# Softmax scores of 640 columns: 384 + 256 columns with two short ones to a bank, in place of 512 + 128 with four to a bank

## The chip, the cores and the metric

The kernel runs on one core of one Trainium2 chip. The metric is the device time of one execution in microseconds (us), the median of the runs shown. Below, PE is the matrix engine, PEld its weight loads, DVE the vector engine, ACT the scalar engine, POOL the GpSimd engine and SP the engine that issues most DMAs.

## The reference

One layer of an encoder on 2048 tokens of width 1024: a normed and modulated input, one projection, eight stick-breaking heads and eight softmax heads of 64 columns, an output projection, and a squared-ReLU MLP. The change is in the softmax heads, whose reference is, cut to what matters:

```python
s = jnp.einsum('bnqhd,bnkhd->bnhqk', qc, k_band).astype(jnp.float32) * (d ** -0.5)
bias = rel_bias[:, rel_idx].astype(jnp.float32)
s = s + bias[None, None]
s = jnp.where(valid[None, :, None, None, :], s, NEG_INF)
p = jax.nn.softmax(s, axis=-1)
out = jnp.einsum('bnhqk,bnkhd->bnqhd', p.astype(v.dtype), v_band)
```

A chunk has 64 queries and sees its own chunk and the 8 before it, 576 keys.

## The kernel before, in words

The kernel handles the tokens in reverse, and takes two chunks as one query tile of 128 rows. Such a tile sees a window of 640 keys (`WIN`), of which the bias masks the corner that each chunk does not see. Near the end of the reversed sequence fewer keys are left.

**Units.** The attention stage walks over units of four query tiles, one tile to a step. A softmax unit, class `CA`, is one head and one group of 512 queries; it is written (head, group) here. Groups 0, 1 and 2 have 640 keys for each of their four tiles. In group 3 the tiles have 512, 384, 256 and 128 keys. The units of groups 1, 2 and 3 of all heads run in one stretch of the program, those of group 0 in a later one, and stick-breaking units (`SB`) before and after the first stretch.

**Scores.** A query tile's scores are a matmul of 640 columns, done twice into the same place since the keys are kept as a high and a low part in one contraction and the query's two parts follow one another (`for l in range(2)`). A PSUM bank holds 512 fp32 columns, so the scores are split: the first `hn` columns go to a bank of the tile's own (names that begin with `cz`), the rest, here called the short part, to a bank that several tiles share (`ct`, `self.tails`). In the kernel before, `hn` is 512, the short part 128, and one `ct` bank takes the short parts of all four tiles, at the start of the unit (L972 to L978).

**What reads the banks.** DVE adds the bias to the short part and takes its minimum (`tail`, L992; the signs are turned, so it is the maximum of the scores), then does the same with the first `hn` columns from that minimum on (L1003). Each of the two is followed by a short instruction that reads the minimum out. ACT takes the exponentials of the 640 columns of SBUF with their sum, DVE the reciprocal, POOL scales.

**The rest of a step.** Eight steps later PE transposes the weights of that unit (`wt`), ACT and DVE split them into a high and a low part (`wth`, `wtl`), and PE multiplies them with the values (`acc`), some steps later still. Between the scores and the next step's transposes, PE gets fill matmuls of other layers' projections (`pf`, `po`), a share that is set by a credit for each step and not by the time.

**Order.** PE's instructions are kept in the order in which the program writes them (`Ordered`); so a PE instruction that waits holds back all that follows. In a step PE's order is transposes, values, the next tile's scores, fill. The other engines and the DMA queue are ordered by the scheduler of the framework, which also picks the bank of each tile. `cz`, `ct`, `wt` and the stick-breaking scores `z` share four PSUM banks (`pz`, tag `z`); a tile takes a bank that has come free and waits, on PE, for the instruction that frees it. In the profile nearly all lines are L42, since a helper records every operation, so names of tiles tell the work apart.

Of the kernel before, what the change touches and what calls it, by code (L numbers as in the profile page):

```python
# [9 lines left out]
F32 = mybir.dt.float32  # L10
# [8 lines left out]
P = 128  # L19
# [6 lines left out]
TB = 512  # L26
# [53 lines left out]
def encoder_kernel(ctx, tc, xT, x3, wf, c, g1, g2, w_in, w_rest, gqk, bias, w_o, w1, w2, w_ada, b_ada, out):  # L80
    nc = tc.nc
    act, dve, pool, sp = nc.scalar, nc.vector, nc.gpsimd, nc.sync
    pe = Ordered(tc, nc.tensor)
    osp = Ordered(tc, nc.sync)

    WIN = 640
# [8 lines left out]
    pz = ctx.enter_context(tc.tile_pool(name="pz", bufs=4, space=PSUM))  # L95
# [36 lines left out]
    def column(tag):  # L132
        small[tag].append(small[tag].pop(0))
        return small[tag][-1]
# [110 lines left out]
    if True:  # L245
# [304 lines left out]
        t = np_.tile([P, 4], F32, tag="nt", name="nta3")  # L550
# [200 lines left out]
    if True:  # L751
# [109 lines left out]
        class SB(Unit):  # L861
# [31 lines left out]
            def scores(self, qi):  # L893
                nm = f"{self.nm}_{qi}"
                c0 = qi * P if self.diag else 0
                n = TB - c0
                self.z = z = pz.tile([P, TB], F32, tag="z", name=f"z{nm}")
                qs = slice(qi * P, (qi + 1) * P)
                pe.matmul(z[:, :n], self.q[:, 0, qs], self.k[:, c0:], start=True, stop=False)
                pe.matmul(z[:, :n], self.q[:, 1, qs], self.k[:, c0:], start=False, stop=True)  # L900
# [28 lines left out]
        class CA(Unit):  # L929
# [34 lines left out]

            def size(self, qi):
                n = min(WIN, self.nk - qi * P)
                return n, min(n, TB)

            def scores(self, qi):
                nm = f"{self.nm}_{qi}"  # L970
                n, hn = self.size(qi)
                if qi == 0 and n > hn:  # L972
                    self.tails = pz.tile([P, TB], F32, tag="z", name=f"ct{nm}")
                    for i in range(STEPS):
                        t = self.tails[:, i * P : (i + 1) * P]
                        ks = slice(i * P + TB, i * P + WIN)
                        for l in range(2):
                            pe.matmul(t, self.q[:, l, i * P : (i + 1) * P], self.k[:, ks], start=l == 0, stop=l == 1)  # L978
                self.z = z = pz.tile([P, TB], F32, tag="z", name=f"cz{nm}")
                ks = slice(qi * P, qi * P + hn)  # L980
                for l in range(2):
                    pe.matmul(z[:, :hn], self.q[:, l, qi * P : (qi + 1) * P], self.k[:, ks], start=l == 0, stop=l == 1)

            def tail(self, qi):
                nm = f"{self.nm}_{qi}"
                n, hn = self.size(qi)
                s = zp.tile([P, WIN], F32, tag="p", name=f"s{nm}")
                m = 3e38
                if n > hn:
                    m = column("m0")  # L990
                    t = self.tails[:, qi * P : (qi + 1) * P]
                    dve.tensor_tensor_reduce(s[:, hn:n], t, self.bt[:, hn:n], -1.0, 3e38, ALU.add, ALU.min, m)  # L992
                self.sm[qi] = (s, m)

# [214 lines left out]
        STEPS = 4  # L1209
# [153 lines left out]
    if True:  # L1363
# [381 lines left out]
        for mb in (1, 0):  # L1745
            begin = len(steps)
            steps += [First(mb, j, i) for j in range(NP) for i in PRODUCTS]
            for j in range(NP):
                f = steps[begin + 7 * j]
# [124 lines left out]
```

## Time and profile before

| | |
|---|---|
| median of 3 runs | 2577.99 us (2572.71 to 2578.78) |
| profiled execution, its own time | 2573.47 us |
| its span, first to last instruction | 2571.7 us |
| granted clock of PE | 1.00 |
| share of the span in which PE, DVE, ACT, POOL are busy | 99%, 73%, 54%, 35% |
| first stretch with softmax units | 564.6 to 763.0 us of the span |
| second stretch with softmax units | 1189 to 1262 us of the span |

A row of the order of time has the start in us, the length in us from the first start to the last end of the instructions merged in it, the engine, the line, the operation, what it writes and reads, the size, and the count; in brackets is the engine's idle time before it and what ended that. The records of matmuls overlap, since each includes its latency; so the distance between the starts of two rows tells how long PE was taken up. A row of a group has, after the bar, the busy time in us and the mean length of one instruction in ns, then the idle time before them. A row of the list of waits has who waited for whom, the total in us, how often, and the longest.

### The profile page before, as it was taken

To read this page: it belongs to the slowest core of one execution; us is meant where nothing else is said; L and a number is where in the kernel's file an instruction comes from. 1 tells how busy PE (TensorE), PEld (TensorE's weight loads), DVE (VectorE), ACT (ScalarE), POOL (GpSimd) and SP (SyncE) were. 2 spreads that over 40 slices of the span, in tenths; PEclk is the share of its full clock that TensorE was granted. 3 is DMA by queue.
4 is the path that set the end of the run, shared out by engine and by line. 5 is a ranking of instruction groups with operands and counts; after the bars stand their busy time and mean duration, and the time that the engine had idled before them with its cause. 6 is when DMAs were issued, how large, how long until landed. Compare 5 with 4: busy or idle time off the path is not lost. (4 is left out here: it accounts for less than half of the span.)

```text
span 2571.7 us, 39222 instructions
## 1 busy us (share of the span) xinstructions
PE 2558.5 (99%) x12851; PEld 2153.6 (84%) x12851; DVE 1870.9 (73%) x3102; ACT 1394.8 (54%) x2596; POOL 904.3 (35%) x1232
## 2 busy tenths in 40 slices
PE   9999999999999999999999999999999999999999
PEld 7888888888889988888888888888888888888887
DVE  7656767887778999998687777768766565645655
ACT  7323434678886666666754444556444444544443
POOL 4330244766666666676513332100003323100000
PEclk9999999999999999999999999999999999999999
DMA  9879887789977686767787767866764344465574
GB/s 396 341 280 371 316 321 254 239 273 273 283 241 228 201 277 195 234 201 225 220 334 258 269 244 276 326 249 225 253 240 149 138 171 144 156 242 196 199 272 151
DMA packets 251263, 633.90 MB, mean 246 GB/s; under 512 B 28209, under 2 KB 56881, under 8 KB 241202
## 3 DMA queue, kind: packets, MB, share of 16 engines
q1 hardware_dynamic: 249760, 626.67, 70.7%
q10 hardware_dynamic: 1298, 4.72, 0.5%
q8 instruction: 101, 1.65, 0.3%
q14 instruction: 104, 0.85, 0.1%
HBM read 439.92 MB, written 191.37 MB: 245 GB/s over the span
## 5 line engine op out<-in xcount | busy, mean ns | idle before, releaser
L42 PE MATMUL ps<-oph,opv 128*128 128x512 f32 x2688 | 612.1, 389 | 0.2
L42 PE MATMUL ps<-h,opw 128*128 128x512 f32 x2664 | 604.2, 389 | 0.0
L42 PEld LDWEIGHTS ps<-oph,opv 128*128 128x128 f32 x2688 | 503.8, 188 | 106.5 <-DVE opv L42 1.2
L42 PEld LDWEIGHTS ps<-h,opw 128*128 128x128 f32 x2664 | 500.0, 188 | 103.9 <-DVE cx L42 0.2
L42 POOL TENSOR_TENSOR b<-p 128x512 f32<-128x512 f32 (+1 forms) x320 | 291.9, 912 | 201.8 <-DVE p L42 119.0
L42 ACT CAST wth<-wt 128x512 fp32r<-128x512 f32 (+1 forms) x432 | 244.1, 567 | 173.7 <-PE wt L42 169.5
L42 DVE TENSOR_TENSOR wtl<-wt,wth 128x512 fp32r<-128x512 f32 (+1 forms) x432 | 280.5, 653 | 63.9 <-ACT wth L42 62.9
L42 DVE TENSOR_TENSOR oph<-hw,oph 128x512 fp32r<-128x512 f32 x224 | 156.7, 699 | 211.4 <-ACT oph L42 211.4
L42 PE MATMUL pt<-w,ht 128*128 128x512 f32 x1248 | 288.0, 391 | 0.0
L42 ACT CAST oph<-hw 128x512 fp32r<-128x512 f32 x224 | 139.3, 622 | 273.5 <-PE ps L42 268.4
L42 POOL TENSOR_TENSOR ts<-w 128x512 f32<-128x512 f32 x32 | 47.2, 1474 | 661.8 <-DMA w<-in_w_dram 601.4
L42 PEld LDWEIGHTS pt<-w,ht 128*128 128x128 f32 x1248 | 233.0, 188 | 47.5
L42 DVE TENSOR_TENSOR_SCAN p<-z,p,zero 128x512 f32<-128x512 f32 x192 | 245.8, 1281 | 32.2 <-ACT z L42 21.3
L42 PE MATMUL acc<-wth,v 128*128 128x512 f32 (+3 forms) x544 | 217.3, 404 | 0.0
L42 ACT ACTIVATE z<-z 128x512 f32<-128x512 f32 (+1 forms) x320 | 165.9, 520 | 62.8 <-PE z L42 58.8
L42 PE MATMUL z<-k,q 128*128 128x512 f32 (+3 forms) x640 | 183.5, 368 | 2.4 <-DVE p L42 2.0
L42 PE MATMUL acc<-wtl,v 128*128 128x512 f32 (+3 forms) x544 | 181.2, 347 | 0.0
L42 DVE TENSOR_TENSOR opw<-w,opw 128x512 fp32r<-128x512 f32 x127 | 96.5, 762 | 113.2 <-ACT opw L42 113.1
L42 POOL TENSOR_TENSOR e<-e,cols 128x640 f32<-128x640 f32 (+1 forms) x128 | 143.0, 1121 | 93.5 <-DVE cols L42 71.9
L42 PE MATMUL wt<-ident,b 128*128 128x128 f32 x1088 | 166.0, 272 | 1.5 <-DVE wtl L42 0.7
L42 PE MATMUL po<-fx,ow 128*128 128x512 f32 x576 | 162.0, 393 | 0.0
L42 PEld LDWEIGHTS wt<-ident,b 128*128 128x128 f32 x1088 | 132.7, 140 | 28.7 <-DVE wtl L42 2.3
(200 smaller groups left out, 4088.9 us busy)
## 6 DMA issues: line engine op xcount, KB each, us to landing
hw<-scr_hid SPq DMA_DIRECT2D x112, 512.0 KB, 3.8
q<-scr_q SPq DMA_DIRECT2D x128, 256.0 KB, 4.7
w<-in_w_dram SPq DMA_DIRECT2D x64, 512.0 KB, 5.3
hw<-scr_s SPq DMA_DIRECT2D x64, 512.0 KB, 4.6
fw<-scr_w SPq DMA_DIRECT2D x28, 1024.0 KB, 7.2
k<-scr_k SPq DMA_DIRECT2D x224, 128.0 KB, 4.1
v<-scr_v SPq DMA_DIRECT2D x112, 256.0 KB, 4.0
wa<-in_w_ada_dram SPq DMA_DIRECT2D x48, 512.0 KB, 7.8
```

What stands on the lines that cost most here:

```text
L42: return lambda *x, **y: self.tc.keep_in_program_order(f(*x, **y))
```

## The change

`hn` becomes 384 where a tile has more than 512 keys. The short part is then 256 columns wide, and a bank holds those of two tiles. So a unit of groups 0, 1 and 2 takes two `ct` banks: the first ahead of the scores of tile 0, the second right behind the scores of tile 1. Tiles with 512 keys or fewer (group 3) are as before.

```diff
             def size(self, qi):
                 n = min(WIN, self.nk - qi * P)
-                return n, min(n, TB)
+                return n, n if n <= TB else 3 * P

             def scores(self, qi):
                 nm = f"{self.nm}_{qi}"
                 n, hn = self.size(qi)
                 if qi == 0 and n > hn:
-                    self.tails = pz.tile([P, TB], F32, tag="z", name=f"ct{nm}")
-                    for i in range(STEPS):
-                        t = self.tails[:, i * P : (i + 1) * P]
-                        ks = slice(i * P + TB, i * P + WIN)
-                        for l in range(2):
-                            pe.matmul(t, self.q[:, l, i * P : (i + 1) * P], self.k[:, ks], start=l == 0, stop=l == 1)
+                    self.ends(0)
                 self.z = z = pz.tile([P, TB], F32, tag="z", name=f"cz{nm}")
                 ks = slice(qi * P, qi * P + hn)
                 for l in range(2):
                     pe.matmul(z[:, :hn], self.q[:, l, qi * P : (qi + 1) * P], self.k[:, ks], start=l == 0, stop=l == 1)
+                if qi == 1 and n > hn:
+                    self.ends(2)
+
+            def ends(self, qi):
+                self.tails = pz.tile([P, TB], F32, tag="z", name=f"ct{self.nm}_{qi}")
+                for i in range(qi, qi + 2):
+                    t = self.tails[:, (i - qi) * 2 * P : (i - qi + 1) * 2 * P]
+                    ks = slice((i + 3) * P, i * P + WIN)
+                    for l in range(2):
+                        pe.matmul(t, self.q[:, l, i * P : (i + 1) * P], self.k[:, ks], start=l == 0, stop=l == 1)

             def tail(self, qi):
...
                 if n > hn:
                     m = column("m0")
-                    t = self.tails[:, qi * P : (qi + 1) * P]
+                    t = self.tails[:, qi % 2 * 2 * P : (qi % 2 + 1) * 2 * P]
                     dve.tensor_tensor_reduce(s[:, hn:n], t, self.bt[:, hn:n], -1.0, 3e38, ALU.add, ALU.min, m)
```

Below is how the instructions stand in three places. In the names, the two or three numbers after the letters are the head, the group and the tile (or the bank of transposes) of the unit; the last number only counts tiles. Stick-breaking names have the key block as well.

PE in unit (2, 1), from the values of the step of tile 0 to the transposes of the next step; before:

```order
L42 MATMUL acc_1_1_7012<-wtl_1_1_2_6973,v_1_1_2_6713 128x128
L42 MATMUL cz_2_1_1_7055<-k_2_1_6797,q_2_1_6794 128x512 x2
L42 MATMUL pf_2_0_6933<-fx_3_6575,fw_2_0_6578 128x512 x2
L42 MATMUL pf_2_0_6933<-fx_4_6892,fw_2_1_6743 128x512
L42 MATMUL wt_1_2_1_7061<-ident,e_1_2_0_6811 128x128
```

and with the change:

```order
L42 MATMUL acc_1_1_7016<-wtl_1_1_2_6977,v_1_1_2_6716 128x128
L42 MATMUL cz_2_1_1_7055<-k_2_1_6796,q_2_1_6793 128x384 x2
L42 MATMUL ct_2_1_2_7058<-k_2_1_6796,q_2_1_6793 128x256 x4
L42 MATMUL pf_2_0_6937<-fx_3_6577,fw_2_0_6580 128x512 x2
L42 MATMUL pf_2_0_6937<-fx_4_6896,fw_2_1_6746 128x512
L42 MATMUL wt_1_2_1_7066<-ident,e_1_2_0_6810 128x128
```

Four `ct` matmuls, the short parts of tiles 2 and 3, now stand between the scores of tile 1 and the fill; the fill itself is the same.

PE in unit (0, 0), the first after stick-breaking units in the second stretch, at the same place, with the waits named; before:

```order
L42 MATMUL cz_0_0_1_15133<-k_0_0_14879,q_0_0_14876 128x512 [waits DVE_49]
L42 MATMUL cz_0_0_1_15133<-k_0_0_14879,q_0_0_14876 128x512
L42 MATMUL po_0_15065<-fx_3_14813,ow_0_14548 128x512 x3
L42 MATMUL po_0_15065<-fx_4_15027,ow_0_14548 128x512 [waits DMAHW1_49]
L42 MATMUL po_0_15065<-fx_4_15027,ow_0_14548 128x512 x2
L42 MATMUL po_0_15065<-fx_5_15029,ow_0_14548 128x512 [waits DMAHW3_49]
L42 MATMUL po_0_15065<-fx_5_15029,ow_0_14548 128x512 x2
L42 MATMUL wt_7_0_2_1_15145<-ident,b_7_0_2_0_14886 128x128 [waits DVE_49]
```

and with the change:

```order
L42 MATMUL cz_0_0_1_15145<-k_0_0_14895,q_0_0_14892 128x384 [waits DVE_49]
L42 MATMUL cz_0_0_1_15145<-k_0_0_14895,q_0_0_14892 128x384
L42 MATMUL ct_0_0_2_15148<-k_0_0_14895,q_0_0_14892 128x256 [waits DVE_49]
L42 MATMUL ct_0_0_2_15148<-k_0_0_14895,q_0_0_14892 128x256 x3
L42 MATMUL po_0_15081<-fx_3_14829,ow_0_14564 128x512 x3
L42 MATMUL po_0_15081<-fx_4_15043,ow_0_14564 128x512 [waits DMAHW1_49]
L42 MATMUL po_0_15081<-fx_4_15043,ow_0_14564 128x512 x2
L42 MATMUL po_0_15081<-fx_5_15045,ow_0_14564 128x512 [waits DMAHW3_49]
L42 MATMUL po_0_15081<-fx_5_15045,ow_0_14564 128x512 x2
L42 MATMUL wt_7_0_2_1_15162<-ident,b_7_0_2_0_14902 128x128 [waits DVE_49]
```

The wait for DVE that stood behind the nine fill matmuls, at the transposes, now stands ahead of them, at the second `ct`; in both programs it is for `wtl_7_0_2_0`, and the transposes wait for the main reduction of tile 0 instead.

DVE in unit (2, 1), from its first instruction on (ISA stands for the addition with its minimum, and for the reading of the minimum that follows); before:

```order
L42 ISA s_2_1_0_7038,cols<-ct_2_1_0_7017,bias_2_1_6798 128x128
L42 ISA cols 128x1
L42 ISA s_2_1_0_7038,cols<-cz_2_1_0_7026,bias_2_1_6798,cols 128x512
L42 ISA cols 128x1
L42 ISA s_2_1_1_7041,cols<-ct_2_1_0_7017,bias_2_1_6798 128x128
```

and with the change:

```order
L42 ISA s_2_1_0_7038,cols<-ct_2_1_0_7021,bias_2_1_6797 128x256
L42 ISA cols 128x1
L42 ISA s_2_1_0_7038,cols<-cz_2_1_0_7026,bias_2_1_6797,cols 128x384
L42 ISA cols 128x1
L42 ISA s_2_1_1_7041,cols<-ct_2_1_0_7021,bias_2_1_6797 128x256
```

DVE has the same instructions in the same order, with other widths. ACT and POOL are unchanged in order; on SP the loads of the softmax and the following stick-breaking units are issued in a somewhat different order.

## The prediction

> **What bounds the kernel now.** I read the page first, then the busy time by stage, the list of waits on PE, and last the order of time inside the softmax stage, the only one that the change touches.
>
> ```profile
> span 2571.7 us, 39222 instructions
> PE 2558.5 (99%) x12851; PEld 2153.6 (84%) x12851; DVE 1870.9 (73%) x3102; ACT 1394.8 (54%) x2596; POOL 904.3 (35%) x1232
> ```
>
> PE is covered for all but 13 us of the span. A share of 99% alone proves little, since a matmul's record includes its latency, so the stage itself has to show it:
>
> ```profile
> 564.60:763.00 198.40, 197.87 (x1231) 173.20 (x1232) 152.37 (x526) 164.95 (x361) 130.01 (x117) 1.00 0.88 270
> ```
>
> ```profile
> 1189.00:1262.00 73.00, 73.00 (x457) 63.86 (x456) 59.54 (x201) 55.83 (x114) 46.62 (x41) 1.00 0.78 222
> ```
>
> These are the two stretches with softmax heads (columns: length, then PE, PEld, DVE, ACT, POOL busy, granted clock, DMA share). PE has no gap worth naming, DVE is busy 77% and 82%, ACT 83% and 76%, the clock is full. The list of PE's waits names only two in these stretches, with the times that each came:
>
> ```profile
> PE wt L42 <- DVE wtl L42: 0.7, 2, 0.5
> PE cz L42 <- DVE wtl L42: 0.5, 1, 0.5
> ```
>
> So time taken off PE here should come off the span, except where PE then meets a later engine. DMA is among no PE wait of that list, which is why I cost the changed order of DMA issues at nothing.
>
> **The change, part by part.** The edit acts in 24 units (8 heads, query groups 0, 1, 2) of four query tiles; I name a unit (head, group). Engines see this per unit: eight ct matmuls of 128 columns become 4+4 of 256, eight cz matmuls of 512 become eight of 384, and the four DVE reductions of each kind change width. Columns and instructions stay the same in number; only the width of each differs. What a matmul costs PE is the distance from start to start, not the duration of its record:
>
> ```profile
> 621.47 1.00 PE L42 MATMUL ct<-k,q 128*128 128x128 f32 x8
> 622.31 0.69 PE L42 MATMUL cz<-k,q 128*128 128x512 f32 x2
> 622.83 0.86 PE L42 MATMUL pf<-fx,fw 128*128 128x512 f32 x3
> 623.53 0.63 PE L42 MATMUL cz<-k,q 128*128 128x512 f32 x2
> 623.99 0.39 PE L42 MATMUL pf<-fx,fw 128*128 128x512 f32 x1
> ```
>
> Eight ct take 622.31-621.47 = 0.84 us, 0.105 each. Two cz take 623.99-623.53 = 0.46; right behind the ct they take 622.83-622.31 = 0.52, because the pace of weight loads, one for each matmul, is still to be paid off. One more pair in a unit stands behind 128-wide matmuls (acc) and takes 614.97-614.45 = 0.52 (next fence). A unit now: 0.84 + 2 x 0.52 + 2 x 0.46 = 2.80 us.
>
> Widths 256 and 384 are both in the trace, beside other work:
>
> ```profile
> 774.85 1.60 PE L42 MATMUL pf<-fw,fx 128*128 128x256 f32 x12
> 776.28 0.60 PE L42 MATMUL wt<-ident,e 128*128 128x128 f32 x4
> ```
>
> Twelve 256-wide ones take 776.28-774.85 = 1.43, 0.119 each: hardly more than a 128-wide one, since the weight load fits under the stream.
>
> ```profile
> 605.51 0.52 PE L42 MATMUL cz<-k,q 128*128 128x384 f32 x2
> 605.87 0.39 PE L42 MATMUL pf<-fx,fw 128*128 128x512 f32 x1
> ```
>
> A 384 pair takes 605.87-605.51 = 0.36. The worst row for a 256 pair is that of tile 2 in group 3, behind 128-wide acc:
>
> ```profile
> 633.32 0.45 PE L42 MATMUL cz<-k,q 128*128 128x256 f32 x2
> 633.60 0.40 PE L42 MATMUL pf<-fx,fw 128*128 128x512 f32 x1
> ```
>
> It takes 0.28 instead of 0.24. A unit after: 8 x 0.119 + 4 x 0.36 + 0.05 (the pair behind the acc keeps its extra) = 2.44, a gain of 0.36. Rows of two decimals leave +-0.04; a pair at 0.35 gives 0.40. I take **0.38 us a unit**, 24 x 0.38 = 9.1 us. The low end is that last pair: at its price the ct cost 4 x 0.28 = 1.12, the unit gains 0.19, and all 4.6 us. I take the row of twelve, for the new ct stand behind 512- or 384-wide matmuls. The high end is 24 x 0.40 = 9.6.
>
> DVE keeps its work:
>
> ```profile
> L42 DVE CUSTOM_DVE_ANT_0 s<-cz,bias,cols 128x512 f32<-128x512 f32 x96 | 71.5, 745 | 5.4 <-PE cz L42 3.5
> L42 DVE CUSTOM_DVE_ANT_0 s<-ct,bias 128x128 f32<-128x128 f32 x96 | 27.6, 287 | 3.4 <-PE ct L42 2.7 <-DMA q<-scr_q 0.2
> L42 DVE CUSTOM_DVE_ANT_0 s<-cz,bias 128x512 f32<-128x512 f32 x8 | 5.5, 690 | 0.9 <-PE cz L42 0.5
> L42 DVE CUSTOM_DVE_ANT_0 s<-cz,bias 128x384 f32<-128x384 f32 x8 | 4.4, 548 | 0.0
> L42 DVE CUSTOM_DVE_ANT_0 s<-cz,bias 128x256 f32<-128x256 f32 x8 | 3.3, 414 | 0.0
> ```
>
> A tile costs 745 + 287 = 1032 ns now. After: 548 + 55 (745-690, for the start value in cols) + 414 = 1017. Nothing to book; were DVE to pace the stage, the gain would go.
>
> **The second bank** is the added wait. ct of tiles 2 and 3 needs a bank right behind the cz of tile 1, ahead of the fill matmuls, and every fill, transpose and value matmul queues behind it. In the built program it waits in 14 units for the main reduction of tile 0 (which frees that tile's cz bank), in the other ten for an older wtl. A plain unit, (2, 1):
>
> ```profile
> 611.91 1.00 PE L42 MATMUL ct<-k,q 128*128 128x128 f32 x8
> 612.75 0.68 PE L42 MATMUL cz<-k,q 128*128 128x512 f32 x2
> 613.27 0.39 PE L42 MATMUL pf<-fx,fw 128*128 128x512 f32 x1
> ...
> 614.45 0.68 PE L42 MATMUL cz<-k,q 128*128 128x512 f32 x2
> 614.97 0.85 PE L42 MATMUL pf<-fx,fw 128*128 128x512 f32 x3
> ```
>
> And DVE in the same unit:
>
> ```profile
> 611.41 1.30 DVE L42 TENSOR_TENSOR wtl<-wt,wth 128x512 fp32r<-128x512 f32 x2 [0.39 <-ACT wth L42]
> 612.95 0.29 DVE L42 CUSTOM_DVE_ANT_0 s<-ct,bias 128x128 f32<-128x128 f32 x1 [0.23 <-PE ct L42]
> 613.47 0.75 DVE L42 CUSTOM_DVE_ANT_0 s<-cz,bias,cols 128x512 f32<-128x512 f32 x1 [0.22 <-PE cz L42]
> 614.14 0.08 DVE L42 DVE_READ_ACCUMULATOR2_ANT cols<- 128x1 f32 x1
> ```
>
> Counted from the first ct: PE gets to the second ct after 0.48 + 0.36 (first ct, cz 0), 614.45-613.27 = 1.18 (unchanged work) and 0.36 (cz 1), at 2.38. DVE ends its wtl at 611.41+1.30-611.91 = 0.80, then needs 0.41 for the short part, some 0.15 until the main one starts, 0.60 and 0.08: the bank is free at 2.04. Margin 0.34 us: no stall. Fill differs from unit to unit; the margin does not last in four:
>
> ```profile
> 563.46 0.63 PE L42 MATMUL cz<-k,q 128*128 128x512 f32 x2
> 564.61 0.65 PE L42 MATMUL wt<-ident,b 128*128 128x128 f32 x4 [0.52 <-DVE wtl L42]
> ```
>
> That is (0, 1). Unit (0, 0), DVE and then PE:
>
> ```profile
> 1188.20 0.69 DVE L42 TENSOR_TENSOR wtl<-wt,wth 128x512 fp32r<-128x512 f32 x1 [1.50 <-ACT wth L42]
> ```
>
> ```profile
> 1187.79 0.62 PE L42 MATMUL cz<-k,q 128*128 128x512 f32 x2
> 1188.26 2.21 PE L42 MATMUL po<-fx,ow 128*128 128x512 f32 x9
> ```
>
> Both units follow a change of head type. In (0, 0) the second ct waits for the wtl of 1188.20, done at 1188.89. PE and this wtl both come 0.52 us earlier, (0.84+0.52)-(0.48+0.36): PE is ready at 1187.79-0.52+0.36 = 1187.63, the bank at 1188.37. About **0.74 us** are lost, where nine fill matmuls used to cover this wtl. In (0, 1) PE already waits 0.52 us for such a wtl; the waits only change place and I book its 0.38 as lost. Unit (2, 0) finds DVE behind:
>
> ```profile
> 1204.14 1.00 PE L42 MATMUL ct<-k,q 128*128 128x128 f32 x8
> 1205.90 0.28 DVE L42 CUSTOM_DVE_ANT_0 s<-ct,bias 128x128 f32<-128x128 f32 x1
> ```
>
> Its first reduction starts 1.76 us after the ct, 0.96 later than the 0.80 of (2, 1), which uses up that margin of 0.34 and 0.62 more. Since the fill between differs, I take 0.4 for it and for (0, 2), where a wtl is late, together. Lost: 0.74 + 0.38 + 0.4 = 1.5 us.
>
> Sum: 9.1 - 1.5 = **7.6 us**. The profiled execution took 2573.47 us (1.8 outside the span) and would take 2565.9. The median of the runs shown is 4.5 higher, 2577.99, and would be **2570.4**.
>
> **The rivals.** (a) More of it stays: no stall at all, 9.1 to 9.6 us, 2568.4 to 2568.9. For it: PE waits almost nowhere. Against: (0, 0) above. (b) Less stays: the margins of 0.3 us are eaten by DVE or ACT (83% busy), or the 0.28 pair is the price: 0 to 6 us are gained, 2572 to 2578. A transfer belongs here:
>
> ```profile
> fw<-scr_w SPq DMA_DIRECT2D x28, 1024.0 KB, 7.2
> ```
>
> One fill weight issued too late would cost up to its 7.2 us. Against: no such wait now. (c) PE time goes by columns alone: if a 128-wide matmul could be fed at half of 0.119, 0.06, eight ct would cost 0.48 now and 0.95 after, and cz would give 8 x 0.06 back: no change, 2578. The row of 0.84 us for eight speaks against it. [...] (d) Slower: the second bank stalls PE in every unit. It decides once DVE has a wtl and an stf more (0.69 each) ahead of the tile's first reduction: then the bank is free 1.38-0.34 = 1.04 us late, 24 x 1.04 = 25 us are lost against 9.1, and the time is 2594. With one wtl more (0.35 late, 8.4 us) it nearly comes out even. Against: in (2, 1) DVE idles 0.23 us for ct before that reduction.
>
> **How the numbers follow.** My forecast (6 to 9 us gained) has 0.58, (a) 0.16, (b) 0.19, (c) 0.02, (d) 0.05. A difference of 0.3%, 7.7 us, is about what a measurement of this kernel can tell from no change, and my forecast lies on it, so half of its chance goes to each side. Faster: 0.29 + 0.16 = 0.45. Same: 0.29 + 0.19 + 0.02 = 0.50. Slower: 0.05. The range goes from 2563 (9.6 us gained, and a median as far down as the lowest run before, 5.3 us) to 2578 (nothing gained); the forecast's own is 2568 to 2573.
>
> **What would show it.** Right: eight ct of 256 columns in 0.95 us a unit, cz pairs 0.36 apart, the first softmax stretch some 5.5 us and the second some 2 us shorter, the other stretches as before, PE waiting about 0.7 us for a wtl before ct in (0, 0) and hardly elsewhere. Wrong: ct of 0.14 us and more each; idle time on PE before ct in most units, released by DVE cols; or new PE waits on a DMA.

## The result, and the profile after

The changed kernel took 2569.61 us (median of 10 runs, 2564.76 to 2574.00) beside 2576.30 us of the kernel before (10 runs): a ratio of 0.9974, 95% interval 0.9965 to 0.9984. A second set of runs gave 0.9970 (0.9959 to 0.9981). By these ratios 0.26% and 0.30% are gained, 6.7 and 7.7 us of 2576; the forecast was 7.6 us and a time of 2570.4.

The profiled execution, though, hardly differs in span from that of the kernel before (2571.7 us):

```profile
span 2572.2 us, 39216 instructions
```

It was the longest of its ten runs, 2574.00 us. Where the time went is read from windows cut at the same work in each profile: up to the first ct, the first softmax stretch (to the next z), the part between, and the second softmax stretch (to its last cz); behind that the two kernels differ by 0.5 us at most. Columns are as in the prediction: length, then PE, PEld, DVE, ACT, POOL busy, granted clock, DMA share, GB/s. First the kernel before:

```profile
0.00:560.70 560.70, 555.74 (x2815) 468.14 (x2816) 402.08 (x633) 271.67 (x518) 231.43 (x440) 1.00 0.86 311
560.70:762.80 202.10, 201.06 (x1253) 175.66 (x1252) 153.52 (x529) 165.71 (x363) 130.45 (x120) 1.00 0.88 269
762.80:1184.80 422.00, 420.84 (x2515) 363.75 (x2514) 381.75 (x461) 273.97 (x509) 283.09 (x486) 1.00 0.70 225
1184.80:1259.40 74.60, 74.60 (x465) 65.21 (x464) 60.16 (x200) 54.30 (x111) 47.39 (x43) 1.00 0.79 224
```

Then the changed kernel, the same four parts of its first profile:

```profile
0.00:564.60 564.60, 557.04 (x2816) 469.03 (x2817) 402.33 (x633) 271.87 (x519) 231.44 (x440) 1.00 0.86 309
564.60:760.60 196.00, 194.97 (x1252) 174.78 (x1251) 152.21 (x529) 164.90 (x363) 130.35 (x120) 1.00 0.85 259
760.60:1186.70 426.10, 422.79 (x2516) 365.49 (x2515) 382.31 (x461) 274.18 (x509) 283.19 (x486) 1.00 0.71 231
1186.70:1259.50 72.80, 72.00 (x466) 64.76 (x465) 59.52 (x200) 54.07 (x111) 47.25 (x43) 1.00 0.75 230
```

The two softmax stretches are 6.1 and 1.8 us shorter, 7.9 together (7.8 with one more decimal). This execution lost about as much where the edit touches nothing: 3.9 us before the first ct, 4.1 us between the stretches. PE's waits name what stood there (total, times, longest):

```profile
PE wt L42 <- DVE p L42: 3.0, 1, 3.0
PE pf L42 <- DMA fw<-scr_w: 2.2, 1, 2.2
PE ct L42 <- DVE wtl L42: 1.3, 2, 0.6
PE wt L42 <- DVE cols L42: 0.3, 1, 0.3
PE ct L42 <- DVE cols L42: 0.2, 1, 0.2
```

The first two lie outside the softmax stretches. The last three belong to the change: PE waits three times for the second ct bank, and once for the bank of a wt right behind the ct of (0, 1). In a plain unit it does not wait. PE's order of time in unit (2, 1), which answers to the prediction's fence:

```profile
614.44 0.64 PE L42 MATMUL ct<-k,q 128*128 128x256 f32 x4
614.92 0.51 PE L42 MATMUL cz<-k,q 128*128 128x384 f32 x2
615.27 0.40 PE L42 MATMUL pf<-fx,fw 128*128 128x512 f32 x1
...
616.47 0.57 PE L42 MATMUL cz<-k,q 128*128 128x384 f32 x2
616.87 0.64 PE L42 MATMUL ct<-k,q 128*128 128x256 f32 x4
617.34 0.39 PE L42 MATMUL pf<-fx,fw 128*128 128x512 f32 x1
```

Four ct of 256 columns take 0.48 and 0.47 us, 0.95 for the eight; a cz pair takes 0.35, and 0.40 where it stands behind 128-wide acc. The second ct starts 2.43 us after the first, forecast 2.38. DVE's groups are as estimated, 612 + 419 = 1031 ns a tile where it was 1032:

```profile
L42 DVE CUSTOM_DVE_ANT_0 s<-cz,bias,cols 128x384 f32<-128x384 f32 x96 | 58.7, 612 | 4.0
L42 DVE CUSTOM_DVE_ANT_0 s<-ct,bias 128x256 f32<-128x256 f32 x96 | 40.2, 419 | 0.0
```

### The profile page after: what moved, and what is told of

Same layout as the page of the kernel before. It is cut to its first block, busy times and chain, and to the rows that moved or that the text cites. A ratio compares the mean times of both kernels' runs of the same rounds, so it can differ in the third digit from the quotient of the medians.

```text
span 2572.2 us, 39216 instructions
## 1 busy us (share of the span) xinstructions
PE 2553.0 (99%) x12851; PEld 2155.4 (84%) x12851; DVE 1867.0 (73%) x3102; ACT 1394.8 (54%) x2596; POOL 903.1 (35%) x1232
## 4 chain that ended last, share of the span: by engine, by line
PE 91%; DVE 3%; DMA 2%; ACT 2%; issue 1%; POOL 1%; SPq 0%; ACTq 0%; DVEq 0%; POOLq 0%
PE ps L42 47%; PE pt L42 11%; PE acc L42 7%; PE wt L42 6%; PE pf L42 5%; PE z L42 5%; PE po L42 4%; PE pq L42 3%; PE cz L42 2%; PE ct L42 1%; DVE p L42 1%; DMA scr_m<-os 1%; PE px L42 1%; POOL b L42 0%; DVE h L42 0%
```

## The experiments

All results in one table. "Stretches" is the sum of the two softmax stretches in each kernel's profile. It is worth more than the medians here: the two kernels that were profiled twice repeat it to 0.1 us, while their times scatter over 10 us, for a reason found below.

| kernel | median us | ratio to before, 95% | stretches us |
|---|---|---|---|
| before | 2576.30, 2576.76, 2578.80 | 1 | 276.7 |
| changed | 2569.61 | 0.9974 (0.9965 to 0.9984) | 268.8 |
| changed, once more | 2567.79 | 0.9970 (0.9959 to 0.9981) | 268.8 |
| arrangement alone | 2577.38 | 0.9997 (0.9988 to 1.0006) | 279.4 |
| arrangement, ct 256 and cz 512 wide | 2580.31 | 1.0008 (0.9998 to 1.0019) | 278.5 |
| changed, second ct behind the fill | 2565.38 | 0.9964 (0.9950 to 0.9977) | 267.3 |
| the same, once more | 2567.11 | 0.9955 (0.9939 to 0.9971) | 267.3 |
| the same, copy into os on POOL | 2567.43 | 0.9957 (0.9945 to 0.9969) | 267.3 |
| changed, one DVE addition more a unit | 2586.16 | 1.0027 (1.0017 to 1.0038) | 283.1 |
| changed, two DVE additions more a unit | 2603.25 | 1.0096 (1.0083 to 1.0109) | 305.1 |

### The changed kernel again

The first question was whether the 8 us lost outside the softmax code belong to the change.

> The changed kernel once more, unaltered. Its first profile lost 3.9 us ahead of the softmax code (one wait of 2.98 us of PE for DVE p at 474.3) and 4.1 us between the two softmax stretches (2.2 of it PE waiting for a fill weight at 809.5); the two softmax stretches together were 7.8 us shorter. Theory 'scatter': these two waits belong to that one execution, the one slowest of its ten; in a second execution they are under 0.6 us each, the first 563 us and the part between the stretches agree with the kernel before to 1.5 us, and the time is 6 to 8 us below it. Rival 'systematic': the new order of loads makes the weight late in each execution, the wait at 809 recurs with 1.5 us or more, and the gain stays 1 us or more under what the softmax stretches give. Both: first ct of the first stretch to the first z behind it 196 us (before: 202), second stretch 72.8 (before: 74.6).

The same four windows of the second profile:

```profile
0.00:559.40 559.40, 555.16 (x2816) 467.50 (x2817) 401.56 (x633) 271.80 (x519) 231.41 (x440) 1.00 0.87 311
559.40:755.40 196.00, 194.96 (x1252) 174.75 (x1251) 152.16 (x529) 164.97 (x362) 130.32 (x120) 1.00 0.84 259
755.40:1178.10 422.70, 421.21 (x2515) 363.88 (x2514) 381.97 (x461) 273.99 (x509) 283.15 (x486) 1.00 0.73 233
1178.10:1250.90 72.80, 71.99 (x465) 64.71 (x464) 59.47 (x200) 54.04 (x110) 47.25 (x43) 1.00 0.78 230
```

They were scatter: the first part is now 1.3 us shorter than in the kernel before, the part between 0.7 us longer, the stretches as in the first profile. This execution took 2565.22 us; the prediction had put the profiled one at 2565.9. A trace of the rival is left. Two waits on a DMA that the kernel before does not list are there again, small:

```profile
PE pso L42 <- DMA opm<-scr_m: 0.5, 2, 0.3
PE pf L42 <- DMA fw<-scr_w: 0.3, 1, 0.3
```

The fill weight holds PE up between the stretches, at the pf of 802.45; the opm load does so behind the second stretch, from 1293.8 us on. PE's earlier arrival is not the reason for the first: the load is issued 7.0 us before PE would use it in both kernels (at 802.27 for 809.26 in the kernel before, at 794.95 for 801.93 here), but it landed after 6.2 us there and after 7.5 here.

### The arrangement without the widths

```diff
-                return n, n if n <= TB else 3 * P
+                return n, min(n, TB)
 ...
-                    t = self.tails[:, (i - qi) * 2 * P : (i - qi + 1) * 2 * P]
-                    ks = slice((i + 3) * P, i * P + WIN)
+                    t = self.tails[:, (i - qi) * P : (i - qi + 1) * P]
+                    ks = slice((i + 4) * P, i * P + WIN)
 ...
-                    t = self.tails[:, qi % 2 * 2 * P : (qi % 2 + 1) * 2 * P]
+                    t = self.tails[:, qi % 2 * P : (qi % 2 + 1) * P]
```

> Only the arrangement of the change: short parts of two tiles to a bank, the second bank written behind the cz of tile 1; the widths are those of before, 512 and 128. Width theory (the gain comes from 128-wide matmuls, whose pace weight loads set): none of the gain is left, ct 0.105 us and cz pairs 0.46 to 0.52 apart. ct now stands in two runs of four, and each run makes one cz pair behind it 0.52 instead of 0.46, so a unit costs at most 0.06 more than before, 1.4 us; with the waits at the turns the time is 0 to 3 us above the kernel before, ratio 1.000 to 1.0012, first stretch 201 to 204 us. Rival 'arrangement' (writing the second pair of ct later takes work out of a crowded place): 3 us or more of the gain stay, ratio 0.9988 or less, first stretch under 199.

Nothing of the gain is left: ratio 0.9997. The stretches are even longer than in the kernel before:

```profile
566.00:770.00 204.00, 201.18 (x1252) 175.72 (x1251) 152.17 (x529) 165.39 (x363) 130.65 (x120) 1.00 0.85 267
1192.10:1267.50 75.40, 74.88 (x466) 65.11 (x465) 59.59 (x200) 54.38 (x111) 47.40 (x43) 1.00 0.78 222
```

279.4 - 276.7 = 2.7 us. One wait of 1.90 us (cz for a wtl, at 698.72) goes back to ACT, which stood 2.82 us until 695.51 for a late store of os, as described below; the next kernel, with the same arrangement, does not have it. Without it 0.8 us remain, in the expected 0 to 3. The rival "arrangement" is out.

### The price of a width

Now ct is 256 wide while cz stays at 512; 128 of its columns repeat what cz computes, and DVE leaves them out.

```diff
-                return n, n if n <= TB else 3 * P
+                return n, min(n, TB)
 ...
-                    t = self.tails[:, qi % 2 * 2 * P : (qi % 2 + 1) * 2 * P]
+                    t = self.tails[:, qi % 2 * 2 * P + P : (qi % 2 + 1) * 2 * P]
```

> Arrangement of the change, cz 512 wide as before, ct 256 wide: half of each ct repeats columns that cz has too, and DVE reads only its last 128. So 192 matmuls are twice as wide as in the kernel with the arrangement alone, and nothing else differs. Width theory (under a weight load of about 0.11 us the columns are free): each costs 0.119 instead of 0.105, and cz pairs behind ct may fall from 0.52 to 0.46, so a unit pays 8 x 0.014 - 0 to 0.12 = -0.01 to 0.11 us, all 0 to 2.7 us. Rival 'columns alone': 128 columns more cost half of 0.119 us, 192 x 0.06 = 11.4 us, ratio to the kernel with the arrangement alone 1.0044.

PE in unit (2, 1), first with the arrangement alone, then with the wide ct:

```profile
616.94 0.55 PE L42 MATMUL ct<-k,q 128*128 128x128 f32 x4
617.34 0.67 PE L42 MATMUL cz<-k,q 128*128 128x512 f32 x2
```

```profile
619.70 0.63 PE L42 MATMUL ct<-k,q 128*128 128x256 f32 x4
620.16 0.62 PE L42 MATMUL cz<-k,q 128*128 128x512 f32 x2
```

Four ct of twice the width take 0.46 instead of 0.40 us. Added up from the trace, start to start, all ct and cz take 2.4 us more than with the arrangement alone, 12.7 ns for each of the 192 matmuls, inside the 0 to 2.7 us of the width theory. The stretches say 1.0 us (278.5 against 277.5, with the stray wait of 1.90 taken out), the medians 2.9, with intervals of 2 to 3 us each way; "columns alone" asked for 11.4. So 128 more columns are nearly free for a 128-wide matmul here. That the weight load sets this price stays the prediction's reading: each matmul here has one, and no run leaves it out. In the profile before, the weight loads (PEld) for the eight ct at 621.47 start 0.11 us apart, seven of them from 621.47 on and the next cz's at 622.25, where the matmuls take 0.105 each. From this kernel to the changed one only the width of cz and DVE's widths differ, and the stretches fall by 9.7 us.

### The second ct behind the fill

```diff
-                if qi == 1 and n > hn:
-                    self.ends(2)
 ...
             fill(front.weight if front else 0.6, 6 if turned else 0)
+            if i + 1 < len(steps) and u.ca and st == 1 and u.nk > TB:
+                u.ends(2)
```

> Widths as changed; the four ct of tiles 2 and 3 are written behind the step's fill matmuls instead of ahead of them. The new bank gets about 1.2 us more. If the waits for the second bank cost what the profile shows, the wait in (0, 0) of 0.64 us and the 0.17 in (2, 0) go, and the time is 0.5 to 1 us below the changed kernel, by its profile's waits; (0, 1) has no fill at that place and keeps its 0.9. Rival 'DVE late': the short reduction of tile 2 now finds its ct late, DVE idles for ct in many units and ends later, and PE then waits for wtl or cols in the next step: the first stretch is 197 to 201 us instead of 196, the time 1 to 5 us above the changed kernel.

In unit (0, 0) the changed kernel waits ahead of its second ct (PE, order of time):

```profile
1189.09 0.52 PE L42 MATMUL cz<-k,q 128*128 128x384 f32 x2
1190.25 0.74 PE L42 MATMUL ct<-k,q 128*128 128x256 f32 x4 [0.64 <-DVE wtl L42]
```

With the ct behind the fill it does not:

```profile
1188.49 0.52 PE L42 MATMUL cz<-k,q 128*128 128x384 f32 x2
1188.86 2.24 PE L42 MATMUL po<-fx,ow 128*128 128x512 f32 x9
1190.93 0.64 PE L42 MATMUL ct<-k,q 128*128 128x256 f32 x4
```

The stretches fall to 195.9 + 71.4 = 267.3 us, 1.5 less than in the changed kernel and more than the 0.5 to 1 us expected: the waits in (0, 0) and (2, 0) cost 0.80 + 0.32 = 1.12 from start to start, not the 0.81 listed (below); 0.4 are not assigned. (0, 1) keeps its waits, and DVE was not late. The run was repeated:

> The kernel with the second pair of ct behind the fill, unaltered, once more. In its first profile the two softmax stretches took 267.3 us against 268.8 of the changed kernel, PE's waits in (0, 0) and (2, 0) were gone, and its time was 0.06% lower, which that run cannot tell from nothing. 'Real': again 267.0 to 267.7 us in the two stretches, and 1 to 2 us under the changed kernel's 2567.8 to 2569.6 by the median. 'Scatter': 268.5 us or more in the stretches.

The stretches repeat at 267.3, so the 1.5 us are real; the medians, 0.7 to 4 us under those of the changed kernel with overlapping intervals, cannot show them. This is the shortest version of the study.

### How much room the second bank has

Rival (d) said that PE stalls in every unit once DVE is late. So DVE was made late: one or two additions of 128x512, overwritten later, stand ahead of the first reduction of tile 0 in each of the 24 units.

```diff
-            def tail(self, qi):
+            def tail(self, qi, extra=0):
 ...
+                for _ in range(extra):
+                    dve.tensor_tensor(s[:, :TB], self.bt[:, :TB], self.bt[:, P:], op=ALU.add)
 ...
-                    self.tail(0)
+                    self.tail(0, 1 if n > hn else 0)
```

> The changed kernel with one DVE addition of 128x512 more ahead of the first reduction of tile 0 in each of the 24 units; its result is overwritten. It stands for a DVE that is late by one wtl, 0.69 us. Theory of the margin (in 14 units the second bank comes free with the main reduction of tile 0, 0.2 to 0.7 us before PE wants it; in the other ten it hangs on an older wtl): PE waits for DVE cols ahead of ct in most of the 14, 3.7 to 5 us in all, and little more in the other ten; the two softmax stretches 272.5 to 274 us against 268.8. As rival (d) priced it, in all 24 units: 8.4 us, 277. Rival 'DVE has room': it idles for ct and cz anyway and catches up; under 1.5 us, stretches under 270.5.

> The same with two such additions, 1.38 us. Theory of the margin: 13 to 15 us from the 14 units, stretches 282 to 284, as much as the change gained and more, so that the time is 4 to 8 us above the kernel before. As rival (d) priced it, in all 24 units: 25 us, 294. Rival 'DVE has room': under 5 us, stretches under 274.

Groups of DVE and PE's waits with one addition:

```profile
L42 DVE TENSOR_TENSOR s<-bias 128x512 f32<-128x512 f32 x24 | 20.6, 859 | 0.0
PE ct L42 <- DVE cols L42: 5.7, 10, 1.8
PE wt L42 <- DVE cols L42: 2.6, 5, 1.0
```

PE's waits with two:

```profile
PE ct L42 <- DVE cols L42: 20.6, 14, 2.5
PE wt L42 <- DVE cols L42: 8.0, 8, 1.7
```

The mechanism is right: ct waits for cols, with one addition ten times, with two in just 14 units, the 14 whose bank hangs on the main reduction of tile 0. Its size was missed, by the theory of the margin (3.7 to 5 and 13 to 15 us) and by (d)'s price (8.4 and 25): the stretches grew by 14.3 and 36.3 us. Three things were missing. An addition took 0.86 us, not 0.69. The units that I had left out wait too, for the bank of a wt, 2.6 and 8.0 us. And a stall cost more than the wait that is listed. In the changed kernel's fence above, a cz pair ends its turn 0.36 us after its start, so without a wait the ct would start at 1189.45; it starts 0.80 later, while the row says 0.64. The record's tail (the pair's 0.52 us beyond its turn of 0.36), which otherwise runs beside the next matmul, stands alone: some 0.15 us a stall. Behind one stall here the granted clock was lower too (0.86 and 0.72 in two windows of 4 us), and behind two with two additions, as described below. With one addition, 7.9 us of listed waits more, 13 stalls more at 0.15 and 1.7 us of clock make 11.5 of the 14.3. With two, 28.1 us of listed waits, 20 stalls and 3.4 us of clock make 34.5 of the 36.3. The rest I cannot assign. "DVE has room" is out.

### Where the scatter comes from

In the first profile PE's wait of 2.98 us goes back to ACT. It makes the rounded copy of a finished pair of heads into os, which has one buffer; the store of the pair before has to land first (ACT, then PE, of the changed kernel):

```profile
471.31 0.62 ACT L42 CAST os<-o 128x512 fp32r<-128x512 f32 x1 [4.52 <-DMA scr_m<-os]
```

```profile
474.34 0.66 PE L42 MATMUL wt<-ident,b 128*128 128x128 f32 x4 [2.98 <-DVE p L42]
```

That ACT wait differs between executions, and PE's wait near 474 us follows it: 0.59 and none (the changed kernel again), 2.10 and 0.6 (before), 3.93 and 2.4 (wide ct), 4.52 and 2.98 (here), 4.66 and 3.08, 5.09 and 3.55 (second and first profile with the late ct), 5.13 and 3.56 (arrangement alone), 2.89 and 1.36 (two additions). PE's wait is 1.5 us shorter each time. With one addition neither is there: ACT waits for no store, and the store landed after 4.25 us, where it took 8.3 in the changed kernel's first profile. To test it, POOL made the copy.

```diff
-            split(os[:, 0, :], os[:, 1, :], o, pool)
+            pool.tensor_copy(os[:, 0, :], o)
+            pool.tensor_tensor(os[:, 1, :], o, os[:, 0, :].bitcast(F32), op=ALU.subtract)
```

> As the kernel with the second pair of ct behind the fill, and one thing beside: the rounded copy of a finished pair of heads into os, which waits for the store of the pair before (os has a single buffer), is made by POOL instead of ACT. Theory: the waits of 2.4 to 3.6 us of PE for DVE p near 474 us, and the 8 us of lower granted clock behind them, come from ACT standing at that copy until a late store lands; then no profile or time shows them: the part from the first z to the first ct is 153 us, where it was 153 to 160, the median is 1 to 3 us lower than without, and the spread of the runs half as wide. Rival: POOL's own later work (b and the scaling of e) is late by the same 3 us and PE waits for that instead: 155 us or more there, the median as without or above.

The large wait is gone; all that PE waits for between 400 and 560 us is this:

```profile
PE z L42 <- DVE p L42: 1.0, 3, 0.4
PE wt L42 <- DVE wtl L42: 0.2, 1, 0.2
```

The part from the first z to the first ct took 153.9 us (expected 153), the five times span 3.0 us (2566.16 to 2569.12) where the six of the kernel without the edit span 10.0 (2563.36 to 2573.37), and none shows a lowered clock. That is what the theory expects, but it does not prove it: in this profile the store, issued at 464.16, landed after 2.9 us, where it took 4.25 to 8.9 us in the nine others. So it was not late, and what the copy on POOL would do behind a late one is not shown; whether the edit kept it from being late is not known either. Five runs at full clock can be chance too, for seven of the 13 without the edit have it. What shows the cause are the waits above, from the store over ACT to PE. The median did not fall, 2567.43 against 2567.11. In the profile the part between the stretches is 423.9 us, where it was 422.0 before, and the wait for a fill weight has grown to 1.0 us: with the edit the long runs are missing, and the shortest too.

## Why the prediction was right

**The price of the widths** held. Forecast: 2.80 to 2.44 us a unit by the rows, 0.38 taken, 9.1 us in all. Eight ct take 0.95 and a cz pair 0.35, as written. From start to start, ct and cz of the whole kernel take 78.2 us before and 70.8 after, waits included. With each listed wait among them counted with 0.15 us for its stall (one of 0.52 before; 0.64, 0.64, 0.17 and 0.26 after), that is 77.5 and 68.5: 9.0 us. The low end of 4.6, where a ct pair would cost 0.28, is refuted.

**The waits at the turns** were put in the right units and a little too high. (0, 0) lost 0.80 us, forecast 0.74; (2, 0) 0.32, and (0, 2) nothing, forecast 0.4 for both; (0, 1) waits 0.64 and 0.26 where it waited 0.52 and 0.47, so that its 0.38 was not lost. All waits in the stretches, stalls included, grew from 1.3 to 2.3 us: 1.0 where 1.5 was booked. 9.0 - 1.0 = 8.0 against 7.8 measured, forecast 7.6.

**The margin in plain units** held in sign: no wait. Its 0.34 us can be compared in (2, 1), where an addition of 0.86 us left a listed wait of 0.23, 0.38 with the stall: the room was 0.48.

**DVE neutral**: 1031 ns a tile, forecast 1017, before 1032.

**DMA order costed at nothing** is the step that was slightly off. The fill weight now lands behind PE, 0.3 us in the undisturbed profile, and the part between the stretches took 422.7 us where it was 422.0; the opm load costs 0.5 us behind the second stretch. In the two kernels without the width gain the part between took 422.1, with the fill weight landing after 5.6 and 6.0 us. Why it takes 7.5 us in the changed kernel stays open; the order of the loads was not tried by itself.

**The rivals.** (b) with its late DMA came true in one execution by 2.2 us, at 809 us, and 1.7 us of lowered clock behind it, and not as a rule. (c), columns alone, is refuted by the wide ct: 12.7 ns for 128 columns, where it needs some 60. (d) is refuted for this kernel; half a microsecond away it is real, in up to 14 units and not in every one.

The whole: 6.7 and 7.7 us were gained, around the forecast's 7.6. That agreement is partly luck, since the scatter of single runs is larger than the gain; the stretches are what supports it. The time of 2569.61 came near the forecast's 2570.4 also because the median of the kernel before fell from 2577.99 with three runs to 2576.30 with ten.

## What to carry to other kernels

Price a matmul by its distance to the next start at each width, with a new weight load for each one: where narrow ones cost nearly what wider ones cost (here 0.105 us at 128 columns and 0.119 at 256), split rows more evenly rather than into a wide and a narrow part. When an edit adds a wait for a buffer, put the instruction behind work that does not need it, and test the room by making the releasing engine late, since a listed stall cost some 0.15 us more than its row here. Compare an edit stage by stage at the same work, and look at an unaltered repeat before explaining a difference elsewhere.

## What the runs showed of the hardware

**Behind some waits of PE a lower clock was granted.** Behind the wait of 2.98 us in the changed kernel (windows of 4 us; the figure before the last two is the granted clock):

```profile
470.00:474.00 4.00, 1.36 (x6) 0.78 (x5) 1.00 (x1) 2.69 (x6) 1.39 (x2) 1.00 0.03 12
474.00:478.00 4.00, 3.01 (x11) 2.19 (x12) 4.00 (x6) 1.55 (x3) 2.33 (x4) 0.76 0.94 321
478.00:482.00 4.00, 4.00 (x20) 3.31 (x18) 3.00 (x4) 2.06 (x5) 2.34 (x4) 0.81 0.88 240
482.00:486.00 4.00, 4.00 (x27) 3.51 (x26) 3.48 (x7) 2.52 (x7) 3.10 (x7) 1.00 0.48 171
```

(0.24 + 0.19) x 4 = 1.7 us of clock are lost. Cut more closely, it is one piece of 3.41 us at half clock, and a second one follows the wait of 2.2 us for the fill weight:

```profile
476.10:479.52 3.42, 3.41 (x9) 2.72 (x10) 3.42 (x4) 0.95 (x2) 2.33 (x4) 0.50 0.87 268
810.61:814.02 3.41, 3.41 (x15) 3.22 (x14) 1.65 (x2) 2.12 (x4) 0.00 (x0) 0.50 0.77 238
```

Behind 3.08 us of waiting with the late ct it is twice that, (0.41 + 0.44) x 4 = 3.4:

```profile
474.00:478.00 4.00, 2.70 (x8) 2.08 (x9) 4.00 (x5) 1.93 (x4) 2.33 (x5) 0.59 0.69 244
478.00:482.00 4.00, 4.00 (x12) 3.06 (x12) 2.92 (x4) 1.22 (x3) 2.70 (x6) 0.56 0.81 233
```

Behind 1.76 us, with one DVE addition more, it is (0.14 + 0.28) x 4 = 1.7 again:

```profile
1210.00:1214.00 4.00, 2.24 (x11) 1.63 (x10) 3.71 (x14) 1.22 (x3) 1.51 (x2) 0.86 0.93 267
1214.00:1218.00 4.00, 4.00 (x22) 3.78 (x21) 0.82 (x5) 1.33 (x3) 1.25 (x1) 0.72 0.53 134
```

Yet behind 2.11 us with two additions (at 762) the full clock was granted:

```profile
764.00:768.00 4.00, 4.00 (x29) 3.69 (x28) 2.94 (x10) 3.60 (x8) 2.94 (x4) 1.00 0.55 145
```

So 1.7 or 3.4 us of clock were lost at a time, and not behind each idle of about 2 us: in that same profile 2.11 us (to 596.48) and 2.01 us (to 705.99) were followed by 1.7 us each, (0.06 + 0.08) x 12 and (0.01 + 0.13) x 12 in windows of 12 us (587 to 611 and 695 to 719), and the 2.11 us before 762 by none. What sets them apart no run shows.

**The store of os** took from issue to landing 3.0 us in the median of 31 issues and 8.3 at most, by those whose landing the trace tells, in the changed kernel's profile. With a single buffer behind it, that one late landing stands ahead of 2.98 us of waiting on PE and 1.7 of clock. What makes it late was not tried.
